# A two-layer decoder trunk on one core: the shared key's product before the first pooled-input tile, copies of the output stage ahead of weight splits, and three output tiles by ScalarE and an accumulating DMA

## The chip, the cores and the metric

One Trainium2 chip; the program runs on one of its NeuronCores. The time is that of one execution on the device, in microseconds (us). Before the change three timed runs took 782.8, 783.03 and 785.17 us, median 783.03. A further execution, the one that was profiled, took 781.9 us. About 0.3% (2.3 us) is what a measurement of this kernel can tell from no change.

Engine names: PE is TensorE's matmul stream, PEld its weight loads, ACT is ScalarE, DVE is VectorE, POOL is GpSimd, SP is SyncE, which here only issues DMAs.

## The reference

Two layers (DEPTH = 2), 512 tokens and 16 meta tokens ahead of them (T = 528), model width 1024, in float32. Per layer:

```
h = rmsnorm(x)
u_pool, z_pool, c_q, c_kv, k_rope, z_mla, g_pool, g_mla = split(h @ W_in)
y_pool = (PoolMix(u_pool) * silu(z_pool)) @ W_pool_up
y_mla  = (MLA(c_q, c_kv, k_rope) * silu(z_mla)) @ W_mla_up
x = x + (sigmoid(g_pool) * y_pool + sigmoid(g_mla) * y_mla) @ W_out
```

PoolMix subtracts u from causal running means over 2, 4, 8 and 16 tokens (four groups of 128 channels) and multiplies each group by a 128x128 matrix (`pool_w_group`, here `wgr`). MLA is causal attention of 8 heads; its rotary key k_rope (32 channels, here `kr`, weights `wkr`) is shared by all heads. Queries and keys are normalised per head.

## The kernel before, in words

**Layout.** Channels lie on the 128 partitions, tokens along the free dimension. The residual stream is `xb`, 8 tiles of 128x528. A product of full float32 accuracy is made by three fast passes: weight and activation are each split into a rounded high part and the rest, and `mm3` issues high*high, high*low, low*high (lines 192, 195, 196).

**The weight stream.** `stream()` runs through one long list, `plan`, of products of both layers, and cuts each weight into chunks of 512 columns. A chunk is loaded by SP into a tile `raw` (three buffers), ACT copies it, rounded, to `whi` (line 187), and DVE makes `wlo` = raw - whi (line 188). The load, the copy and the difference of a chunk are issued when PE's program has come to three chunks ahead. So the order of `plan` sets three things at once: PE's order, the order of SP's loads, and where the `whi` copies stand among the other work of ACT. Every engine works through its own list in order: an ACT instruction that waits holds up all that stand behind it on ACT.

**The products around the change.** Per layer the plan has cq0 to cq4 (query latents), then u0, k0, u1, kr, k1, u2, k2, u3, k3 (u: pooled input, k: keys of a pair of heads), then v, `yw` (the load and split of `wgr`, no product of its own; `hold` keeps the tiles), the zp and y tiles, cq5, and so on. Each cq and u tile has two weight chunks (c0, c1). The result of a cq tile is taken out of PSUM by ACT (line 714), by DVE (line 715) and by ACT again (a square into `tmp`, line 724), that of u by DVE times the norm `rinv` (line 550), that of k by DVE times `q` (line 749). PSUM banks of the tag `mm` go round four buffers, so a product's first matmul waits until the tile four earlier has been taken out. kr (lines 461 to 490) uses the raw weights with the gain multiplied in by POOL, 32 PE instructions of 32 rows, in two halves of the tokens; after its evacuation its later steps (`rest`) wait LAG of planned time.

**The norm.** `norm_sums` (from line 399) gets the norms of the layer's input as one column, and SP writes them to DRAM in four DMAs (`ndr<-ny`, lines 438 and 439, with one element per run), then reads them back spread over all partitions (`rinv<-ndr`, `q<-ndr`, line 444). These DMAs stand in SP's list between the weight loads.

**The output stage.** For each layer the tiles o0 to o3 are plain products of 8 chunks of K. After each half of the tokens `ev_o` (line 1092) adds 0.5 times the PSUM to `xb` on DVE, and `out` sends it on (in the last layer by a DMA to the output yT on POOL's queue). The other four tiles are made in two pairs (u = 0, 1) by seven half-size products instead of eight, in the order 1, 2, 7, 6, 5 ("oa"), o3, then 4, 3 ("ob"). Products 1, 6, 5 and 3 of a pair add up in one PSUM bank `S` and are read out between: after p = 1, 6 and 5 `carry` (line 1161) copies the bank to a tile `sv` by ACT (line 1163) and adds that to `xb` by an accumulating DMA that POOL issues (line 1164); the next product into the bank waits for that copy.

## Time and profile before

| what | us |
|---|---|
| timed runs, median of three | 783.03 (782.8 to 785.17) |
| the profiled execution | 781.9 |
| its span, first to last instruction | 780.1 |
| PE busy in the span | 773.2 |
| DVE, ACT, POOL busy | 569.7, 444.7, 232.7 |

The granted TensorE clock is 1.00 throughout. A row of a timeline gives start, duration, engine, line, operation, output <- inputs, shape, and in square brackets the idle time of that engine just before it and what ended it. The duration of a matmul row (0.28) is longer than the distance to the next row (0.12): matmuls are pipelined, so the distance counts. SPq and POOLq rows are the issues of DMAs, not their transfers; the DMA views give the time from issue to landing. Tiles are named without their numbers there: `raw`, `whi`, `mm` and so on.

### The profile page before, as it was taken

The numbers are of one execution on the slowest core, as the hardware profiler recorded it, in microseconds if no ns is written. First come the engines' busy times: TensorE is split into PE (matmuls) and PEld (weight loads), VectorE is DVE, ScalarE is ACT, GpSimd is POOL, SyncE is SP. The second block draws the span as 40 slices with busy tenths as digits, with TensorE's granted clock in tenths as the row PEclk, the third lists the DMA queues.
The fourth block names the chain that finished last, engine by engine and source line by source line (L and its number), as shares of the span: only waits on it lengthen the run. The fifth ranks groups of instructions, "written<-read, shape, count | busy, mean of one in ns | idle before, by whom it ended". The sixth has DMA issues, their size and how long they took to land.

```text
span 780.1 us, 15325 instructions
## 1 busy us (share of the span) xinstructions
PE 773.2 (99%) x5469; PEld 710.9 (91%) x5469; DVE 569.7 (73%) x1326; ACT 444.7 (57%) x1016; POOL 232.7 (30%) x303
## 2 busy tenths in 40 slices
PE   9999999999999999999999999999999999999998
PEld 8999899999999999999997898887788999988887
DVE  5848787446778876589764577866897888864994
ACT  7645555645566665645564446546657766664552
POOL 1024525103335333211330136221006625340213
PEclk9999999999999999999999999999999999999999
DMA  6232457765646465565662424425557666662645
GB/s 245 82 96 89 125 171 151 177 168 144 156 110 164 116 141 120 156 156 184 169 171 82 109 75 122 133 62 178 146 132 167 173 187 158 175 226 72 210 137 154
DMA packets 65325, 112.92 MB, mean 145 GB/s; under 512 B 10704, under 2 KB 15696, under 8 KB 65248
## 3 DMA queue, kind: packets, MB, share of 16 engines
q1 hardware_dynamic: 55344, 92.18, 39.1%
q0 software_dynamic: 8896, 17.92, 12.9%
q10 hardware_dynamic: 1008, 1.84, 0.7%
q8 instruction: 43, 0.70, 0.4%
q14 instruction: 34, 0.28, 0.1%
HBM read 100.18 MB, written 22.62 MB: 157 GB/s over the span
## 4 chain that ended last, share of the span: by engine, by line
PE 91%; DVE 4%; DMA 2%; ACT 1%; issue 1%; POOL 0%; DVEq 0%; ACTq 0%; POOLq 0%
PE mm L192 26%; PE mm L196 26%; PE mm L195 25%; PE S L195 3%; PE S L196 3%; PE S L192 3%; PE mm L979 2%; DVE wlo L188 1%; PE o L985 1%; PE o L984 1%; PE S L506 1%; DMA raw<-wgr 1%; DMA xb<-xT 1%; PE mm L408 1%; ACT whi L187 0%
## 5 line engine op out<-in xcount | busy, mean ns | idle before, releaser
L192 PE MATMUL mm<-hh,whi 128*128 128x264 f32 (+2 forms) x992 | 306.2, 311 | 0.5 <-DVE u L550 0.4
L196 PE MATMUL mm<-hh,wlo 128*128 128x264 f32 (+2 forms) x992 | 304.4, 309 | 0.1
L195 PE MATMUL mm<-hl,whi 128*128 128x264 f32 (+2 forms) x992 | 304.1, 308 | 0.0
L188 DVE TENSOR_TENSOR wlo<-raw,whi 128x512 fp32r<-128x512 f32 (+1 forms) x253 | 180.0, 714 | 100.3 <-ACT whi L187 98.0
L187 ACT ACTIVATE whi<-raw 128x512 fp32r<-128x512 f32 (+1 forms) x253 | 154.2, 613 | 168.7 <-PE mm L195 110.2
L192 PEld LDWEIGHTS mm<-hh,whi 128*128 128x128 f32 x992 | 186.2, 188 | 11.3 <-issue 1.0
L195 PEld LDWEIGHTS mm<-hl,whi 128*128 128x128 f32 x992 | 186.8, 188 | 8.7
L196 PEld LDWEIGHTS mm<-hh,wlo 128*128 128x128 f32 x992 | 185.9, 188 | 9.0 <-DVE wlo L188 0.6
L922 POOL TENSOR_SCALAR pa<-pa,rs 128x272 f32<-128x272 f32 (+1 forms) x32 | 33.2, 1038 | 103.3 <-DVE rs L941 64.5
L922 POOL TENSOR_SCALAR cq<-cq,rs 128x400 f32<-128x400 f32 (+1 forms) x32 | 51.2, 1600 | 0.0
L192 PE MATMUL mm<-cq,whi 128*128 128x264 f32 (+2 forms) x140 | 43.8, 313 | 0.0
L195 PE MATMUL mm<-cq,whi 128*128 128x264 f32 (+2 forms) x140 | 43.7, 312 | 0.0
L196 PE MATMUL mm<-cq,wlo 128*128 128x264 f32 (+2 forms) x140 | 43.3, 312 | 0.1
L908 DVE CUSTOM_DVE_ANT_0 S<-S,maskw,nqs 128x272 f32<-128x272 f32 (+4 forms) x80 | 38.6, 498 | 5.3 <-PE S L196 5.0
L725 POOL TENSOR_TENSOR racc<-racc,tmp 128x264 f32<-128x264 f32 (+1 forms) x15 | 14.0, 936 | 85.5 <-ACT tmp L724 85.5
L304 DVE TENSOR_TENSOR tl<-mm,th 128x512 fp32r<-128x512 f32 (+1 forms) x64 | 30.0, 483 | 8.0 <-ACT th L303 6.3
L359 POOL DMA_DIRECT2D wsum<-wout x8 | 7.0, 875 | 91.6 <-PE mm L196 86.9
L303 ACT ACTIVATE th<-mm 128x512 fp32r<-128x512 f32 (+1 forms) x64 | 26.3, 433 | 10.2 <-PE mm L979 9.6
L915 ACT ACTIVATE cq<-S,bia 128x400 f32<-128x400 f32 (+2 forms) x48 | 24.5, 514 | 13.2 <-DVE bia L953 8.5
L192 PE MATMUL mm<-u,whi 128*128 128x264 f32 (+1 forms) x96 | 31.3, 326 | 0.0
L196 PE MATMUL mm<-u,wlo 128*128 128x264 f32 (+1 forms) x96 | 30.9, 322 | 0.0
L195 PE MATMUL mm<-kn,whi 128*128 128x264 f32 (+1 forms) x96 | 30.6, 320 | 0.0
(344 smaller groups left out, 1684.7 us busy)
## 6 DMA issues: line engine op xcount, KB each, us to landing
raw<-win SPq DMA_DIRECT2D x139, 256.0 KB, 2.8
raw<-wout SPq DMA_DIRECT2D x22, 256.0 KB, 3.6
bc<-kdr SPq DMA_DIRECT2D x16, 264.0 KB, 4.5
wsum<-wout SPq DMA_DIRECT2D x16, 256.0 KB, 3.5
raw<-wpu SPq DMA_DIRECT2D x16, 256.0 KB, 2.7
wsumgp<-win SPq DMA_DIRECT2D x16, 256.0 KB, 3.4
raw<-wmu SPq DMA_DIRECT2D x16, 256.0 KB, 2.8
raw<-wsumgp SPq DMA_DIRECT2D x16, 256.0 KB, 4.3
```

The lines of the kernel that those rows point to most:

```text
L187: act.activation(hi[:, :n], raw[:, :n], AF.Copy)
L188: dve.tensor_sub(lo[:, :n], raw[:, :n], hi[:, :n].bitcast(F32))
L192: first = pe.matmul(out, wh, xh, start=start, stop=False, skip_group_check=more)
L195: pe.matmul(out, wh, xl, start=False, stop=False, skip_group_check=more)
L196: newest[0] = pe.matmul(out, wl, xh, start=False, stop=stop, skip_group_check=more)
L303: act.activation(hi[:, a:b], src, AF.Copy)
L304: dve.tensor_sub(lo[:, a:b], src, hi[:, a:b].bitcast(F32))
L725: self.acc_last = gp.tensor_add(self.acc[:, a:b], self.acc[:, a:b], t[:, :b - a])
L908: dve.tensor_tensor_reduce(out=sv, in0=sv, in1=mask, scale=nqs[:, i, h:h + 1], scalar=3e38, op0=ALU.add, op1=ALU.min, accum_out=bia[:, c:c ...
L915: act.activation(pv, sv, AF.Exp, scale=-1.0, bias=bia[:, i:i + 1], accum_out=rs[:, c:c + 1])
L922: gp.tensor_scalar(pt[i], pt[i], rs[:, i:i + 1], None, op0=ALU.mult)
L979: pe.transpose(tr[:, P * (i - j):P * (i - j + 1)], pt[i][:, NM + P * j:NM + P * (j + 1)], ident)
```

## The change

Four edits:

1. **kr** goes from behind u1 to ahead of u0 in the plan of both layers, and its later steps wait KR_LAG = 10500 instead of LAG = 2000 of planned time.
2. **yw** goes from behind v to behind u2; `wgr` is loaded into a buffer of the tag `bc` instead of the next `raw`, and its load waits for the newest matmul.
3. **The copies of p = 1** (`kept`, both layers): the second and third `whi` copies recorded after such a copy are made to stand behind it (`urgent`, `behind`). Its accumulating DMA (`join`) is now issued after the addition of p = 2 to the same tile.
4. **o0, o1, o2 of the last layer**: ACT copies 0.5 times the PSUM to a `tmp` tile, and POOL issues an accumulating DMA of it to `xb`, in place of DVE's addition.

```diff
@@ -53,6 +53,7 @@
 FILL = (2950.0, 2700.0)
 RESERVE = ("gm5", "gm5")
 LAG = 2000.0
+KR_LAG = 10500.0
 SPL = 240
 RET = 12500.0
 WARM = 8
@@ -169,8 +170,15 @@
             return self.src[c // 512] if isinstance(self.src, list) else self.src[:, c:c + n]
 
     loads = [0]
+    urgent = []
 
     def wload(src, n, gain, spare, buf=None, held=False):
+        if held:
+            hi, lo = slot("sv", F32R, bufs=2), slot("sv", F32R, bufs=2)
+            raw = slot("bc", bufs=3)
+            behind(sp.dma_start(raw[:, :n], src), newest[0])
+            split(hi, lo, raw[:, :n], 0, n)
+            return hi, lo
         raw = early.pop(0) if early else fetch(src, n, buf or rawt(), sp)
         loads[0] += 1
         pool, th, tl, nb = (tp, "th", "tl", 2) if loads[0] <= 2 or spare else (wp, "whi", "wlo", 3)
@@ -178,13 +186,13 @@
             v = raw[:, :n].rearrange("p (k m) -> p k m", k=8)
             gp.tensor_mul(v, v, gain.unsqueeze(2).to_broadcast([P, 8, n // 8]))
             return raw, None
-        if held:
-            hi, lo = slot("sv", F32R, bufs=2), slot("sv", F32R, bufs=2)
-            split(hi, lo, raw[:, :n], 0, n)
-            return hi, lo
         hi = pool.tile([P, W if pool is tp else 512], F32R, tag=th, name=nm("whi"), bufs=nb)
         lo = pool.tile([P, W if pool is tp else 512], F32R, tag=tl, name=nm("wlo"), bufs=nb)
-        act.activation(hi[:, :n], raw[:, :n], AF.Copy)
+        made = act.activation(hi[:, :n], raw[:, :n], AF.Copy)
+        for e in urgent:
+            e[1] += 1
+            if 1 < e[1] < 4:
+                behind(made, e[0])
         dve.tensor_sub(lo[:, :n], raw[:, :n], hi[:, :n].bitcast(F32))
         return hi, lo
 
@@ -487,7 +495,7 @@
                 act.activation(kr, t[:, :n], AF.Copy, scale=self.g(G_KR))
                 self.rope(self.kp[:, a:b], kr, a, b)
 
-            after(LAG, rest)
+            after(KR_LAG, rest)
 
         def stat(self, q, a, b, c, made):
             for s, (fa, fb) in enumerate(FULL):
@@ -1089,7 +1097,12 @@
         def ev_o(self, m, nxt):
             def ev(ps, a, b):
                 x = xb[:, m, a:b]
-                dve.scalar_tensor_tensor(out=x, in0=ps, scalar=0.5, in1=x, op0=ALU.mult, op1=ALU.add)
+                if self.last and m < 3:
+                    t = tmp()[:, a:b]
+                    act.activation(t, ps, AF.Copy, scale=0.5)
+                    gp.dma_start(x, t, accum_op=ALU.add)
+                else:
+                    dve.scalar_tensor_tensor(out=x, in0=ps, scalar=0.5, in1=x, op0=ALU.mult, op1=ALU.add)
                 self.out(m, (a, b), nxt, gp)
                 if not self.last and m == 3 and b == T:
                     nxt.square_x(m)
@@ -1158,10 +1171,15 @@
                 x = xb[:, m, s[0]:s[1]]
                 dve.scalar_tensor_tensor(out=x, in0=v, scalar=0.5, in1=x, op0=ALU.mult, op1=ALU.add)
 
+            def kept(v, u, scale, o):
+                urgent.append([act.activation(self.carried[u][:, o:o + n], v, AF.Copy, scale=scale), 0])
+
+            def join(m, s, u, o):
+                gp.dma_start(xb[:, m, s[0]:s[1]], self.carried[u][:, o:o + n], accum_op=ALU.add)
+
             def carry(m, s, v, u, scale, o):
-                t = self.carried[u][:, o:o + n]
-                act.activation(t, v, AF.Copy, scale=scale)
-                gp.dma_start(xb[:, m, s[0]:s[1]], t, accum_op=ALU.add)
+                kept(v, u, scale, o)
+                join(m, s, u, o)
 
             def body(i, w):
                 p, u = order[i]
@@ -1180,9 +1198,10 @@
                 q = sp if name == "ob" else gp
                 if p == 1:
                     self.carried[u] = slot("sv", bufs=2)
-                    carry(m0, A, ps, u, 0.5, 0)
+                    kept(ps, u, 0.5, 0)
                 elif p == 2:
                     grow(m0, A, ps)
+                    join(m0, A, u, 0)
                     self.out(m0, A, nxt, q)
                 elif p == 7:
                     grow(m1, B, ps)
@@ -1232,8 +1251,11 @@
                 cq(m)
             for m in range(4):
                 add(f"u{m}", wi(MT_U + m), D, evac=self.ev_u(m), xs=hs, segs=FULL)
-                if m == 1:
-                    add("kr", wkr[l], 256, body=self.kr_body, gain=gn[:, l * N_GAIN + G_H:l * N_GAIN + G_H + 8])
+                if m == 2:
+                    add("yw", wgr[l], 512, body=self.hold)
+                    plan[-1].held = True
+                if m == 0:
+                    plan.insert(-1, Gemm((l, "kr"), wkr[l], 256, body=self.kr_body, gain=gn[:, l * N_GAIN + G_H:l * N_GAIN + G_H + 8]))
                 kk(m)
             def zp(m):
                 add(f"zp{m}", wi(MT_ZP + m), D, evac=self.ev_silu(self.zps, "xa", m), xs=hs, segs=XS)
@@ -1242,8 +1264,6 @@
                 add(f"y{m}", None, P, body=self.y_body(m))
 
             add("v", wvb[l], 1024, body=self.v_body)
-            add("yw", wgr[l], 512, body=self.hold)
-            plan[-1].held = True
             zp(0)
             zp(1)
             y(0)
```

Lines of the changed file lie further down by 1 to 22 (whi copies 191, wlo 196, the cq evacuation 722, 723 and 732, kr 473, `rest` 492 on, the p = 1 copies 1175, o copies 1102).

What this makes of the order is shown at three places. In the names the first number counts the tiles of the program and the second the order of creation. The first place is SP's list in layer 0, around the norm's writes. Here raw_115 is chunk c1 of cq4. Before, raw_120 and raw_127 are u0's chunks c0 and c1:

```order
L115 DMA raw_115_706<-win 128x512
L115 DMA raw_120_738<-win 128x512
L438 DMA ndr00_115<-ny2_76_461 128x4x1
L439 DMA ndr00_115<-ny2_76_461 16x1
L438 DMA ndr01_116<-ny2_76_461 128x4x1
L439 DMA ndr01_116<-ny2_76_461 16x1
L115 DMA raw_127_780<-win 128x512
L444 DMA rinv_78_480<-ndr00_115 128x528
L444 DMA q1_79_481<-ndr01_116 128x528
L115 DMA raw_132_812<-wkb 128x256
```

Now, with u0's chunks as raw_125 and raw_134, and k0's as raw_139:

```order
L116 DMA raw_115_706<-win 128x512
L116 DMA raw_120_738<-wkr 128x256
L446 DMA ndr00_115<-ny2_76_461 128x4x1
L447 DMA ndr00_115<-ny2_76_461 16x1
L446 DMA ndr01_116<-ny2_76_461 128x4x1
L447 DMA ndr01_116<-ny2_76_461 16x1
L116 DMA raw_125_777<-win 128x512
L452 DMA rinv_78_480<-ndr00_115 128x528
L452 DMA q1_79_481<-ndr01_116 128x528
L116 DMA raw_134_813<-win 128x512
L116 DMA raw_139_845<-wkb 128x256
```

The load of kr's weights has taken the place ahead of the norm's writes; u0's two chunks have each moved one load back, u0's first chunk to behind the writes, and u0's second to behind the norm's reading back.

The second place is ACT's list at the same point of the program. mm_104 and mm_105 are the two halves of cq3, mm_118 and mm_119 those of cq4. Before:

```order
L724 ACTIVATE tmp_113_686<-mm_104_634 128x264
L187 ACTIVATE whi_121_740<-raw_120_738 128x512
L714 ACTIVATE cq6_111_682<-mm_105_635,gn_76 128x264
L724 ACTIVATE tmp_114_703<-mm_105_635 128x264
L187 ACTIVATE whi_128_782<-raw_127_780 128x512
L714 ACTIVATE cq8_123_756<-mm_118_712,gn_76 128x264
L724 ACTIVATE tmp_125_760<-mm_118_712 128x264
L187 ACTIVATE whi_133_814<-raw_132_812 128x256
L714 ACTIVATE cq8_123_756<-mm_119_713,gn_76 128x264
L724 ACTIVATE tmp_126_777<-mm_119_713 128x264
```

Now:

```order
L732 ACTIVATE tmp_113_686<-mm_104_634 128x264
L191 ACTIVATE whi_126_779<-raw_125_777 128x512
L722 ACTIVATE cq6_111_682<-mm_105_635,gn_76 128x264
L732 ACTIVATE tmp_114_703<-mm_105_635 128x264
L191 ACTIVATE whi_135_815<-raw_134_813 128x512
L722 ACTIVATE cq8_121_753<-mm_118_712,gn_76 128x264
L732 ACTIVATE tmp_123_757<-mm_118_712 128x264
L191 ACTIVATE whi_140_847<-raw_139_845 128x256
L722 ACTIVATE cq8_121_753<-mm_119_713,gn_76 128x264
L732 ACTIVATE tmp_124_774<-mm_119_713 128x264
L484 ACTIVATE tmp_131_794<-mm_128_783 128x264
L484 ACTIVATE tmp_133_808<-mm_132_799 128x264
```

The evacuations of cq3's second half and of cq4 keep their places; the `whi` copies ahead of each of them are now of a load that stands one further back in SP's list, and kr's own evacuation (L484) follows behind them all. On PE the halves of kr (mm_128, mm_132) and of u0 (mm_137, mm_138) take the PSUM banks of mm_104, mm_105, mm_118 and mm_119 in this order, so they wait for tmp_113, tmp_114, tmp_123 and tmp_124.

The third place is ACT's list in the last layer's output stage, around the copies of p = 1 (S_1959 and S_1964 before, S_1962 and S_1967 now). Before:

```order
L187 ACTIVATE whi_1971_10084<-raw_1970_10082 128x512
L303 ACTIVATE sq_1914_9831<-cq4_1871_9599 128x256
L187 ACTIVATE whi_1975_10105<-kh_1974_10103 128x512
L187 ACTIVATE whi_1983_10145<-kl_1982_10143 128x512
L303 ACTIVATE sq_1918_9835<-cq5_1872_9601 128x256
L303 ACTIVATE sq_1922_9839<-cq6_1856_9557 128x256
L187 ACTIVATE whi_1979_10125<-raw_1978_10123 128x512
L1163 ACTIVATE sv_1960_10036<-S_1959_10023 128x256
L1163 ACTIVATE sv_1965_10058<-S_1964_10045 128x256
L303 ACTIVATE rinv_1926_9843<-cq7_1876_9627 128x256
L187 ACTIVATE whi_1986_10165<-raw_1985_10163 128x512
```

Now, where kl_1969 holds the weights of p = 2 for u = 1, raw_1973 and kh_1977 those of p = 7, and mm_1954 is o2:

```order
L1102 ACTIVATE tmp_1958_10019<-mm_1954_9976 128x512
L311 ACTIVATE rinv_1926_9843<-cq7_1876_9627 128x256
L1175 ACTIVATE sv_1963_10042<-S_1962_10029 128x256
L1175 ACTIVATE sv_1968_10063<-S_1967_10050 128x256
L191 ACTIVATE whi_1970_10067<-kl_1969_10065 128x512
L191 ACTIVATE whi_1974_10089<-raw_1973_10087 128x512
L191 ACTIVATE whi_1978_10111<-kh_1977_10109 128x512
L191 ACTIVATE whi_1982_10131<-raw_1981_10129 128x512
```

Before, the two copies stood behind the weights of p = 7 (whi_1971, whi_1975) and of p = 6 (whi_1983, whi_1979); now they stand ahead of those (whi_1974, whi_1978, whi_1982) and of p = 2 for u = 1 (whi_1970), and behind the copy of o2.

## Prediction on record

> **What bounds the kernel now.** The page's busy times first, then the waits of PE:
>
> ```profile
> PE 773.2 (99%) x5469; PEld 710.9 (91%) x5469; DVE 569.7 (73%) x1326; ACT 444.7 (57%) x1016; POOL 232.7 (30%) x303
> ```
> ```profile
> PE S L192 <- ACT sv L1163: 1.1, 1, 1.1
> PE mm L192 <- DVE u L550: 0.8, 2, 0.4
> ```
>
> PE works in 773.2 of 780.1 us and waits in very few places. So an edit can win only what PE waits for there, and can lose whatever new wait it puts into a stream that has hardly any. Where PE waits, by its timeline:
>
> ```profile
> 58.09 0.28 PE L196 MATMUL mm<-kh,wlo 128*128 128x264 f32 x1
> 58.80 0.36 PE L192 MATMUL mm<-hh,whi 128*128 128x264 f32 x1 [0.42 <-DVE u L550]
> ...
> 83.58 0.40 PE L196 MATMUL mm<-whi,kl 128*128 128x512 f32 x1
> 84.38 0.50 PE L192 MATMUL mm<-whi,kh 128*128 128x512 f32 x1 [0.41 <-DVE u L550]
> ...
> 476.03 0.40 PE L196 MATMUL mm<-whi,kl 128*128 128x512 f32 x1
> 476.48 0.50 PE L192 MATMUL mm<-whi,kh 128*128 128x512 f32 x1
> ...
> 755.73 0.28 PE L196 MATMUL mm<-hh,wlo 128*128 128x256 f32 x1
> 757.08 0.39 PE L192 MATMUL S<-cq,whi 128*128 128x256 f32 x1 [1.07 <-ACT sv L1163]
> ```
>
> Distances count, less the usual one (0.12 us for 264 or 256 columns, 0.23 for 512): u1 loses 0.59 us, v 0.57 in layer 0 and 0.21 in layer 1, p = 6 of the last output stage 1.23. **Together 2.6 us: that is all the change can win, 0.33%.** The stall at 84.38 hangs on the load of wgr, as the chain of waits shows:
>
> ```profile
> 79.42 2.87 DMA raw<-wgr
> ```
>
> **Edit 1, kr ahead of u0, layer 0.** PE's work itself stays: kr takes 2.0 us wherever it stands.
>
> ```profile
> 64.86 1.99 PE L465 MATMUL mm<-xb,raw 128*32 128x264 f32 x32
> ```
>
> But every weight load from u0 on moves one place back in SP's list, and this is past the norm's writes. SP and ACT there:
>
> ```profile
> 38.93 0.33 SPq L115 DMA_DIRECT2D raw<-win  x1
> 40.10 0.39 SPq L438 DMA_DIRECT2D ndr<-ny  x1
> ...
> 42.15 0.37 SPq L115 DMA_DIRECT2D raw<-win  x1
> ...
> 49.88 0.32 SPq L444 DMA_DIRECT2D q<-ndr  x1
> 50.29 0.38 SPq L115 DMA_DIRECT2D raw<-wkb  x1
> ```
> ```profile
> 47.05 0.39 ACT L724 ACTIVATE tmp<-mm 128x264 f32<-128x264 f32 x1 [1.02 <-DVE cq L715]
> 52.54 0.63 ACT L187 ACTIVATE whi<-raw 128x512 fp32r<-128x512 f32 x1 [5.10 <-DMA raw<-win]
> 53.08 0.47 ACT L714 ACTIVATE cq<-mm,gn 128x264 fp32r<-128x264 f32 x1
> 54.40 0.39 ACT L724 ACTIVATE tmp<-mm 128x264 f32<-128x264 f32 x1 [0.85 <-DVE cq L715]
> 54.69 0.41 ACT L187 ACTIVATE whi<-raw 128x256 fp32r<-128x256 f32 x1
> ```
>
> The load issued at 42.15, right behind the writes, is not there before 52.5, 10.4 us later, and ACT stands still for 5.1 us. The writes, of single elements, need 8.6 us from issue to landing themselves:
>
> ```profile
> ndr<-ny SPq DMA_DIRECT2D x2, 2.0 KB, 8.6
> ```
>
> Today this costs PE nothing: the late load is u0's second chunk, and cq3 has left its PSUM bank by 47.44, ahead of the hold. After the change the late load is u0's **first** chunk, its copy stands on ACT ahead of the second evacuation of cq3, and kr's second half needs that bank. With the row distances above moved to the new order:
> - PE ends cq4 at 50.79, where u0 starts today:
>
> ```profile
> 50.79 0.28 PE L192 MATMUL mm<-hh,whi 128*128 128x264 f32 x1
> ```
>
> - kr's first half runs 50.9 to 51.85 (its bank was free long ago). The copy of u0's first chunk starts at 52.54, the evacuation of cq3 behind it ends at 54.79 (54.40 + 0.39). kr's second half starts at 54.9: **3.0 us of PE idle**.
> - u0's second chunk is issued at 50.29 and lands at 54.3, as the load issued at 50.29 does today:
>
> ```profile
> DMA to landing us min/median/max: 4.0/4.0/4.0
> ```
>
>   Its copy goes 54.9 to 55.5, then cq4's first half is taken out: today's stretch from the start of a whi copy to the end of the tmp behind it is 52.54 to 54.79, 2.25 us, so 57.1. kr ended at 55.85: **1.3 us idle** before u0.
> - k0's load waits for the raw buffer of u0's first chunk (DVE's difference ends near 53.9), lands near 57; copy and evacuation of cq4's second half (2.25 us again, less 0.2 since the copy is 256 wide, 0.41 against 0.63) end near 59.1. u0's first twelve matmuls, 0.12 apart, end at 58.6: **0.5 us**.
>
> Together 4.8 us; the 0.59 us of u1 goes (ACT has caught up, some 3 us, when u1 starts): **+4.2 us**. Bounds: -0.59, if the load lands by 49.6 (51.85 less 2.25), and +6, if it lands 1.8 us later still.
>
> **Edit 1, layer 1.** The same list, with all of the evacuation in one piece of 512:
>
> ```profile
> 435.34 0.37 SPq L115 DMA_DIRECT2D raw<-win  x1
> ```
> ```profile
> 444.45 0.94 ACT L187 ACTIVATE whi<-raw 128x512 fp32r<-128x512 f32 x2 [3.35 <-DMA raw<-win]
> 445.30 0.67 ACT L714 ACTIVATE cq<-mm,gn 128x512 fp32r<-128x512 f32 x1
> 446.90 0.60 ACT L724 ACTIVATE tmp<-mm 128x512 f32<-128x512 f32 x1 [0.93 <-DVE cq L715]
> ```
>
> Here cq4 ends at 443.98 and kr finds free banks: 444.0 to 446.0. u0's first half waits for cq3's evacuation, now behind the copy at 444.45: about 2.7 us on (its copy 0.54, then 445.30 to 447.50 as shown, less the second copy), 447.15: 1.15 us idle. Its second half waits for cq4's, behind the copy of k0's weights, whose load can be issued only when DVE has used the late chunk, near 445.85. The view of the loads issued from 445.8 to 446.7 has one of this size whose landing it shows, that of wkr:
>
> ```profile
> DMA to landing us min/median/max: 3.1/3.1/3.1
> ```
>
> So 448.9, and 2.5 us from the k0 copy (near 445.0 today) to 447.50, gives 451.4 at most; with a landing after 2.0 us 450.4. u0's first twelve end at 448.6: 1.8 to 2.8 us idle, taken as 2.15. **+3.3 us**, bounds 0 and +4.2.
>
> **Edit 2, yw.** wgr takes 2.87 us to land (the chain's row above) and is now asked for after u2's first chunk. Its split stands on ACT ahead of u3's second chunk, which PE needs 60 matmuls later (24 of u2, 12 of k2, 24 of u3), 7.2 us. Both stalls at v go: **-0.78 us**; at worst as much comes back (0).
>
> **Edits 3 and 4, last output stage.** ACT's copies of p = 1 come late because they stand behind a whi copy that waits; PE's last matmul of the banks, then ACT:
>
> ```profile
> 754.52 0.28 PE L196 MATMUL S<-hh,wlo 128*128 128x256 f32 x1
> ```
> ```profile
> 756.12 0.63 ACT L187 ACTIVATE whi<-raw 128x512 fp32r<-128x512 f32 x1 [1.57 <-PE mm L196]
> 756.66 0.64 ACT L1163 ACTIVATE sv<-S 128x256 f32<-128x256 f32 x2
> ```
>
> With the banks complete near 754.7, the copies put in front end at 755.4, and the 1.23 us go; but now the weights of p = 2 (u = 1) are copied behind them, 755.4 to 756.05, and are wanted at 755.85, their differences 0.65 later, and those of p = 7 follow as closely: 0.7 us come back. On PE -0.5. Then POOL: three accumulating DMAs of 0.88 us issue more, and each output DMA behind waits for their landing (median 3.5 us at half the size):
>
> ```profile
> xb<-sv POOLq DMA_DIRECT2D x6, 128.0 KB, 3.5
> ```
> ```profile
> 764.97 0.88 POOL L1164 DMA_DIRECT2D xb<-sv  x1
> ...
> 774.27 0.56 POOL L1101 DMA_DIRECT2D yT<-xb  x1 [1.04 <-DMA xb<-sv]
> ```
> ```profile
> 773.41 4.32 SPq L1101 DMA_DIRECT2D yT<-xb  x4
> ```
>
> One after the other (o1 asked for near 751.3, three such rounds of 4 to 6 us, then p = 5's two, o3's output last) they bring POOL's last output issue from 774.3 to about 777.4, just where SP's last issue is today (773.41 plus 4.32 us for four). So POOL takes the 0.5 us back: **0**, bounds -1.2 and +2.5. DVE's three additions of 0.68 us that go stood beside other work. In layer 0's output stage, where PE has no wait now, the new order is taken at **+0.3** (0 to +1).
>
> **Sum.** 4.2 + 3.3 - 0.8 + 0 + 0.3 = +7.0 us. The profiled execution (span 780.1, 781.9 in all, the rest as before) becomes 788.9. It was 1.1 us below the median of the timed runs, 783.03, from which it would be 790.0. I say **789.0**, nearer to the first, whose rows made the sum.
>
> **The rivals.**
> - *The load isn't held, faster.* If u0's first chunk lands like others (the page's median for raw<-win is 2.8 us) before 49.6 in layer 0 and 443.3 in layer 1, ACT is in time everywhere, all four stalls go and 781.9 - 2.6 = **779.3**. Against: two loads in exactly this place took 10.4 and 9.1 us. For: other orders of the same bytes haven't been seen. 12%.
> - *Only one layer pays.* Layer 1's kr finds its banks free, so it has 2 us more than layer 0; if the loads there land 3 us sooner, its 3.3 go and **785.6** remains; half of both holds gives 781.9 + 7.5/2 - 0.5 = 785.2, a third 783.9. Together, with the case that little moves (781 to 783: the new waits in the output stages eat what yw gives), 18%.
> - *PE slows after the idle.* At the start of the span PE's matmuls of 264 columns are still 0.22 us apart, instead of 0.12:
>
> ```profile
> 5.71 0.42 PE L195 MATMUL S<-hl,whi 128*128 128x264 f32 x1
> 5.93 0.34 PE L196 MATMUL S<-hh,wlo 128*128 128x264 f32 x1
> ```
>
>   If an idle of 3.0 us brings that back for as long as at the start (1.0 to 5.9), 4.9 x (1 - 0.12/0.22) = 2.2 us more: **791.2**, from an idle that long on. The longest idle in mid-run today, 1.07 us at 757.08, has no such aftermath. 12%. The Trainium skill, "TensorE: Matmul & The Clock Gate", section "HAM oscillation — how this bites in real kernels", warns of idle gaps over about 3.4 us, after which the clock is halved; by it a gap of 3.0 us, followed after 1 us of narrow matmuls by one of 1.3, lies at the edge. The page's granted clock of 1.00 even at the start doesn't show it; the distances do.
>
> **How the numbers follow.** The forecast with its own range 785.5 to 791 has 58%; the slow PE 12%; little or half the loss 18%; the free load 12%. Faster by over 0.3% (under 780.7): 0.12. Within 0.3%, about what a measurement can tell from no change: 0.18. Slower (over 785.4): 0.70. The range leaves out the free load and the ends of the others: 782.0 to 792.5.
>
> **What would show it.** Right: ACT idle some 5 us to a DMA raw<-win near 52.5, with the cq evacuation behind it; PE idle near 3 us in the middle of kr, near 55, and again before u0, both ended by ACT's tmp; in layer 1 two waits within u0, at 447 and 451; no wait at v; p = 6 without its 1.1 us, and POOL's issues ending near SP's. Wrong: u0's first load landing before 50, or PE's idle put down to POOL or to kr's own weights.

## The result, and the profile after

The changed kernel took **791.69 us** (median of six runs, 790.14 to 794.54), beside 782.91 us (six runs, 781.74 to 785.17) for the kernel before. The ratio is **1.0113 [1.0091, 1.0135]**: 8.8 us slower, 7.1 to 10.6 by the interval. The forecast of 789.0 had the sign, 7.0 of the 8.8 us, and the place. The profiled execution of after is the slowest of its six, 794.54 us with a span of 792.5; some of what follows in its trace is therefore its own, and is named as such.

The page's busy times of after. PE does the same 5469 instructions, and its share falls from 99% to 98%; ACT has three copies more and DVE three additions less.

```profile
PE 778.2 (98%) x5469; PEld 714.0 (90%) x5469; DVE 565.9 (71%) x1323; ACT 447.4 (56%) x1019; POOL 233.8 (30%) x306
```

PE's waits in after (total, times, longest). What stood here before, the waits for `sv` and for `u`, is gone or small; in their place PE waits for ACT's `tmp`, the evacuation of cq:

```profile
PE mm L200 <- ACT tmp L732: 4.6, 3, 2.3
PE mm L473 <- ACT tmp L732: 2.0, 1, 2.0
PE mm L987 <- POOL pa L930: 1.2, 1, 1.2
...
PE mm L200 <- DVE u L558: 0.3, 1, 0.3
```

SP's list in layer 0 of after. The load at 43.33 is u0's first chunk, directly behind the four writes of the norm; `q` is read back only at 51.53, and u0's second chunk is asked for behind it, at 51.95.

```profile
40.12 0.33 SPq L116 DMA_DIRECT2D raw<-wkr  x1
41.28 0.38 SPq L446 DMA_DIRECT2D ndr<-ny  x1
...
42.73 0.50 SPq L447 DMA_DIRECT2D ndr<-ny  x1
43.33 0.37 SPq L116 DMA_DIRECT2D raw<-win  x1
49.10 0.33 SPq L452 DMA_DIRECT2D rinv<-ndr  x1
51.53 0.32 SPq L452 DMA_DIRECT2D q<-ndr  x1
51.95 0.38 SPq L116 DMA_DIRECT2D raw<-win  x1
54.24 0.33 SPq L116 DMA_DIRECT2D raw<-wkb  x1
```

ACT at the same place: 6.58 us idle until that load is there, and then each evacuation of cq (L732) one behind a weight copy (L191) that came late.

```profile
45.89 0.39 ACT L732 ACTIVATE tmp<-mm 128x264 f32<-128x264 f32 x1 [0.62 <-DVE cq L723]
52.86 0.63 ACT L191 ACTIVATE whi<-raw 128x512 fp32r<-128x512 f32 x1 [6.58 <-DMA raw<-win]
53.39 0.46 ACT L722 ACTIVATE cq<-mm,gn 128x264 fp32r<-128x264 f32 x1
54.71 0.39 ACT L732 ACTIVATE tmp<-mm 128x264 f32<-128x264 f32 x1 [0.85 <-DVE cq L723]
56.24 0.63 ACT L191 ACTIVATE whi<-raw 128x512 fp32r<-128x512 f32 x1 [1.14 <-DMA raw<-win]
...
58.09 0.39 ACT L732 ACTIVATE tmp<-mm 128x264 f32<-128x264 f32 x1 [0.85 <-DVE cq L723]
```

PE: kr is cut into two halves, with 2.00 us idle between them and 2.28 us behind them. Then the first matmuls of u0 follow each other after 0.39 and 0.22 us, not after 0.12.

```profile
52.06 1.10 PE L473 MATMUL mm<-xb,raw 128*32 128x264 f32 x16
55.15 1.10 PE L473 MATMUL mm<-xb,raw 128*32 128x264 f32 x16 [2.00 <-ACT tmp L732]
58.53 0.59 PE L200 MATMUL mm<-hh,whi 128*128 128x264 f32 x1 [2.28 <-ACT tmp L732]
58.92 0.42 PE L203 MATMUL mm<-hl,whi 128*128 128x264 f32 x1
59.14 0.42 PE L204 MATMUL mm<-hh,wlo 128*128 128x264 f32 x1
```

The windows of the same stretch (busy time and count of PE, PEld, DVE, ACT and POOL, then the granted clock, the DMA share and GB/s). The clock is 0.50 for the 3 us after the second idle, and back at 1.00 from 62 on:

```profile
55.10:58.50 3.40, 1.10 (x16) 0.42 (x16) 1.09 (x2) 1.41 (x5) 0.75 (x1) 0.98 0.15 51
58.50:60.00 1.50, 1.47 (x6) 1.47 (x7) 1.18 (x2) 0.66 (x2) 0.75 (x1) 0.50 0.50 175
60.00:61.00 1.00, 1.00 (x7) 1.00 (x6) 0.20 (x2) 0.85 (x3) 0.32 (x1) 0.50 0.11 43
61.00:62.00 1.00, 1.00 (x7) 1.00 (x7) 0.97 (x3) 0.11 (x1) 0.43 (x1) 0.60 0.86 305
62.00:63.00 1.00, 1.00 (x10) 1.00 (x9) 0.97 (x4) 0.00 (x0) 0.00 (x0) 1.00 0.13 45
```

Layer 1: kr runs in one piece, and u0 waits twice, ahead of its first half and ahead of its second. The clock stays at 1.00 here.

```profile
450.87 1.99 PE L473 MATMUL mm<-xb,raw 128*32 128x264 f32 x32
454.65 0.39 PE L200 MATMUL mm<-hh,whi 128*128 128x264 f32 x1 [1.79 <-ACT tmp L732]
...
458.32 0.39 PE L200 MATMUL mm<-hh,whi 128*128 128x264 f32 x1 [0.56 <-ACT tmp L732]
```

How much each place costs is read by pairing each PE instruction of after with the same one of before and taking the difference of their starts, in the two profiled executions. It grows by 1.3 us in the first 10 us of the span (PE's matmuls stay 0.22 us apart to 10.5 us instead of 6); by 5.0 at kr and u0 of layer 0, the 0.59 us that u1 no longer waits included; it falls by 0.6 at v; grows by 0.2 up to the attention, by 0.9 in layer 0's output stage, by 3.3 at kr and u0 of layer 1; falls by 0.2 at v; grows by 1.2 at one attention step that waited for POOL (line 987 above), by 0.6 up to 662, and by 0.2 in the last output stage. Together 12.0; the span grew by 12.4. Without the start and the attention's wait, 9.5 remain, near the 8.8 of the medians; both are taken for chance. The profile of the kernel with u0's weights ahead (below) has the same attention wait at no loss, and a kernel with all four edits and constant products (below) has 0.2 us there; the profile of the kernel with edits 1 and 2 and u0's weights ahead has the same slow start, also at no loss.

### The profile page after: what moved, and what is told of

Same layout as the page of the kernel before. It is cut to its first block, busy times and chain, and to the rows that moved or that the text cites. A ratio compares the mean times of both kernels' runs of the same rounds, so it can differ in the third digit from the quotient of the medians.

```text
span 792.5 us, 15331 instructions
## 1 busy us (share of the span) xinstructions
PE 778.2 (98%) x5469; PEld 714.0 (90%) x5469; DVE 565.9 (71%) x1323; ACT 447.4 (56%) x1019; POOL 233.8 (30%) x306
## 4 chain that ended last, share of the span: by engine, by line
PE 86%; DVE 5%; DMA 4%; ACT 2%; issue 2%; POOL 1%; SPq 0%; DVEq 0%; ACTq 0%
PE mm L200 24%; PE mm L204 24%; PE mm L203 24%; PE S L203 2%; PE S L204 2%; PE S L200 2%; PE mm L987 2%; DVE wlo L196 2%; PE o L993 1%; DMA ndr<-ny 1%; PE o L992 1%; DMA raw<-win 1%; ACT whi L191 1%; PE S L514 1%; DMA raw<-wsum 1%
## 5 line engine op out<-in xcount | busy, mean ns | idle before, releaser
L200 PE MATMUL mm<-hh,whi 128*128 128x264 f32 (+2 forms) x992 | 307.6, 313 | 5.5 <-ACT tmp L732 4.6
L196 DVE TENSOR_TENSOR wlo<-raw,whi 128x512 fp32r<-128x512 f32 (+1 forms) x253 | 178.2, 708 | 115.8 <-ACT whi L191 113.7
L191 ACT ACTIVATE whi<-raw 128x512 fp32r<-128x512 f32 (+1 forms) x253 | 154.1, 613 | 164.8 <-PE mm L203 106.6
L200 PEld LDWEIGHTS mm<-hh,whi 128*128 128x128 f32 x992 | 187.2, 190 | 18.2 <-ACT tmp L732 5.8
L930 POOL TENSOR_SCALAR cq<-cq,rs 128x400 f32<-128x400 f32 (+1 forms) x32 | 54.7, 1728 | 0.0
L200 PE MATMUL mm<-cq,whi 128*128 128x264 f32 (+2 forms) x140 | 43.8, 313 | 0.0
L200 PE MATMUL mm<-u,whi 128*128 128x264 f32 (+1 forms) x96 | 31.3, 327 | 0.0
```

The source lines that it names most:

```text
L191: made = act.activation(hi[:, :n], raw[:, :n], AF.Copy)
L196: dve.tensor_sub(lo[:, :n], raw[:, :n], hi[:, :n].bitcast(F32))
L200: first = pe.matmul(out, wh, xh, start=start, stop=False, skip_group_check=more)
L930: gp.tensor_scalar(pt[i], pt[i], rs[:, i:i + 1], None, op0=ALU.mult)
```

## The experiments

Every time is a median beside runs of the kernel before on the same chip (781.47 to 781.74 there). The ratio goes by the means of the runs, so it can differ a little from that of the medians; differences in us are worked out from the ratio. In brackets is its interval.

**Which edit.** First each side of the cut: edit 1 alone, and all but edit 1.

*Edit 1 alone*, on the kernel before:

```diff
-            after(LAG, rest)
+            after(10500.0, rest)
...
-                if m == 1:
-                    add("kr", wkr[l], 256, body=self.kr_body, gain=...)
+                if m == 0:
+                    plan.insert(-1, Gemm((l, "kr"), wkr[l], 256, body=self.kr_body, gain=...))
```

> The kernel before with edit 1 alone. Theory H: 791 to 793, all of the loss plus the 0.8 us that edit 2 would win. Theory O: 786 to 789. In the trace under H: PE idle 2.0 to 3.0 us in the middle of kr and over 2 us ahead of u0 in layer 0, 1.8 and 0.6 us within layer 1's u0, and a granted clock of 0.5 for some 3 us behind the second idle.

Measured 789.86 us, ratio 1.0108 [1.0091, 1.0125], +8.4 us: between the ranges of the two theories, nearer to H. The profile is of the fastest of its four executions, 787.22 us. In it PE waits for the same two things, at the same places (1.42 us in the middle of kr, 2.32 ahead of u0 in layer 0), and the granted clock falls to 0.50 behind them:

```profile
PE mm L192 <- ACT tmp L724: 3.6, 3, 2.3
PE mm L465 <- ACT tmp L724: 1.4, 1, 1.4
```

Edit 1 by itself makes a loss as large as the whole change makes.

*Edit 1 undone*, on the changed kernel (kr behind u1 and LAG again, edits 2 to 4 kept):

```diff
-            after(KR_LAG, rest)
+            after(LAG, rest)
...
-                if m == 0:
-                    plan.insert(-1, Gemm((l, "kr"), wkr[l], 256, body=self.kr_body, gain=...))
+                if m == 1:
+                    add("kr", wkr[l], 256, body=self.kr_body, gain=...)
```

> The change with edit 1 undone: kr behind u1 and its late steps after LAG, as before; edits 2 to 4 stay. Theory H (the loss is edit 1's alone: the held load of u0's first chunk on ACT, then PE): the time falls to 781.5 to 783, since the 0.78 us at v are won and the output stages come out even; no PE wait between 51 and 60 us, ACT's idle of 5 us stays ahead of u0's second chunk. Theory O (part of the loss sits in the output stages or in POOL's accumulating DMAs): 784 to 787. Theory A (the lost time after layer 0's kr is mostly chance of the profiled execution): also near 782.

Measured 783.53 us, ratio 1.0024 [1.0015, 1.0033], +1.9 us. No wait for `tmp` is left. But the other edits were to give 0.5 us, and they lose 1.9; the time lies above the range of theory H. The trace says where: PE's last matmul starts at 777.5 (before: 776.6), and the span goes on to 782.1 (before: 780.1). So 0.9 us are PE's, and 1.1 are the tail behind it: the chain that ends last now runs through POOL, which asks for its last output DMAs only from 776.88 on (before: 774.27), behind the accumulating ones.

```profile
771.67 2.67 POOL L1178 DMA_DIRECT2D xb<-sv  x3
776.88 1.77 POOL L1114 DMA_DIRECT2D yT<-xb  x3 [2.54 <-DMA xb<-sv]
```

**Why edit 1 costs.** The forecast's reason was the load held up behind the norm's writes. Three kernels vary that hold.

*The norm's writes issued by POOL*, so that SP's queue holds only the loads:

```diff
-                sp.dma_start(row[0, NM:T].rearrange("(j p) -> p j", p=P), ny[:, i, 0:4])
-                sp.dma_start(row[0, 0:NM].rearrange("(p j) -> p j", j=1), ny[0:NM, i, 4:5])
+                gp.dma_start(row[0, NM:T].rearrange("(j p) -> p j", p=P), ny[:, i, 0:4])
+                gp.dma_start(row[0, 0:NM].rearrange("(p j) -> p j", j=1), ny[0:NM, i, 4:5])
```

> The change with the four norm writes of each layer issued from POOL instead of SP, so that they stand in another DMA queue than the weight loads; nothing else. Theory Hq (u0's first load is late because it stands behind the small writes in the same queue): it lands within 3 to 5 us of its issue near 41, ACT takes cq3 out before 48, no idle in layer 0's kr, and in layer 1 none ahead of u0: 782 to 785. Theory He (the small writes hold the DMA engines themselves, whichever queue they are in): the load lands near 52 again, and the time stays at 790 to 793.

Measured 806.99 us, ratio 1.0326 [1.0311, 1.0342], +25.5 us, which no theory had. SP, POOL and ACT in layer 0:

```profile
41.15 0.33 SPq L116 DMA_DIRECT2D raw<-win  x1
...
58.20 0.33 SPq L452 DMA_DIRECT2D q<-ndr  x1
58.62 0.38 SPq L116 DMA_DIRECT2D raw<-wkb  x1
```
```profile
40.00 0.91 POOL L446 DMA_DIRECT2D ndr<-ny  x1 [2.36 <-DVE ny L325]
40.90 0.54 POOL L447 DMA_DIRECT2D ndr<-ny  x1
48.11 0.81 POOL L446 DMA_DIRECT2D ndr<-ny  x1 [6.67 <-issue]
```
```profile
50.17 0.63 ACT L191 ACTIVATE whi<-raw 128x512 fp32r<-128x512 f32 x1 [5.47 <-DMA raw<-win]
...
63.54 0.42 ACT L191 ACTIVATE whi<-raw 128x256 fp32r<-128x256 f32 x1 [8.12 <-DMA raw<-wkb]
```

Two things are seen. u0's first chunk, asked for at 41.15, is used only at 50.17, 9.0 us on, though the writes now stand in another queue: so it isn't SP's order that holds the load, but something that the queues share. The bytes themselves are late, not only the sign that they are there. The windows (columns as above) show a load of the same size ahead of the writes, in before (issued at 38.93), then u0's first chunk behind them in after, up to where the next read begins, and the same chunk here:

```profile
39.90:41.20 1.30, 1.30 (x12) 1.30 (x12) 0.54 (x2) 1.27 (x3) 0.76 (x1) 1.00 0.68 202
44.30:51.00 6.70, 6.70 (x57) 6.70 (x56) 1.36 (x2) 0.87 (x2) 1.07 (x2) 1.00 0.31 36
42.10:49.80 7.70, 7.70 (x65) 7.70 (x65) 1.18 (x2) 1.25 (x3) 1.67 (x3) 1.00 0.32 34
```

Ahead of the writes the 256 KB go through in 1.3 us, at 202 GB/s; behind them they trickle in at 36 and 34 GB/s, whichever queue the writes are in.

And a new loss: POOL could not issue the second pair of writes until 48.11, 6.67 us later, in which it waited for nothing that the profile shows; so `q` was read at 58.20 and the weights of k0 behind it came at 63.5. The Trainium skill, "DMA: Bandwidth & Descriptors", section "Queues, rings and completion order", says that the semaphore of a DMA is raised by a write that lands only after every earlier write of the same DMA engine, across its queues. The order of landings here is in keeping with it: the first pair of writes landed 7.8 and 7.1 us after 40.00 and 40.90, ahead of the load. But it is not what the load waited for in the end, since its bytes were still moving until 49.8.

*kr one place later*, between u0 and k0, on the changed kernel:

```diff
-                    plan.insert(-1, Gemm((l, "kr"), wkr[l], 256, body=self.kr_body, gain=...))
+                    add("kr", wkr[l], 256, body=self.kr_body, gain=...)
```

> The change with kr one product later, between u0 and k0, still with KR_LAG; edits 2 to 4 stay. SP's list up to u0's second chunk is then that of the kernel before, and the late load is again the second chunk of u0. Theory H: PE has no idle ahead of u0 and 782 to 784.5 come out. If the loss came from kr standing early as such (its two tmp tiles held for KR_LAG, or DVE's work for it behind u0), it would stay above 787.

Measured 784.66 us, ratio 1.0039 [1.0024, 1.0054], +3.1 us, just above the range of theory H. u0's first chunk is again ahead of the writes; PE's waits for `tmp` of cq are gone, its clock is 1.00, and two small waits stand there instead:

```profile
PE mm L200 <- DVE tmp L486: 1.0, 1, 1.0
PE mm L200 <- ACT whi L191: 0.5, 1, 0.5
```

Moving kr ahead of k0 and u1 costs about 1.2 us beside the same kernel with kr at its old place (ratio 1.0024); moving it ahead of u0 as well costs some 7. The step comes where u0's first chunk goes behind the norm's writes.

*u0's weights ahead of the writes*, with kr where the change puts it. The order of SP's list is what the theory blames, so this takes away the hold of u0's chunks and leaves PE's order: they are loaded ahead of the writes into two tiles that are free then (`u2`, `kn2`), which also spares two of the `raw` buffers.

```diff
+            if g_.name[1] == "u0":
+                early.append(layers[g_.name[0]].pre.pop(0))
...
+            for c, t in ((0, slot("u2", w=WU)), (512, slot("kn2"))):
+                behind(sp.dma_start(t[:, 0:512], win[self.l, MT_U][:, c:c + 512]), mm)
+                self.pre.append(t)
             for i, d in enumerate((self.inv, self.cinv)):
```

> The change with u0's two weight chunks of each layer loaded into two free tiles, with their issue ahead of the norm writes in SP's list; kr stays ahead of u0, all else as in the change. Theory H: the load right behind the writes is now that of k0's weights, ACT takes cq3 and the first half of cq4 out without a hold, PE has no idle in the middle of kr and none ahead of u0, at most 1 us within u0 (the second half of cq4 stands behind k0's copy): 783 to 785.5, close to the change with kr put back (783.5 beside 781.5 of before). If kr ahead of u0 costs by itself (its tmp tiles, DVE's and POOL's work), it stays above 787.

Measured 781.86 us beside 781.66, ratio 1.0005 [0.9996, 1.0014]: the whole loss is gone, and more than theory H expected. PE and ACT in layer 0; the copies of u0's chunks (from `u` and `kn` now) come at 45.35 and 48.30, and kr runs unbroken into u0:

```profile
51.21 1.99 PE L478 MATMUL mm<-xb,raw 128*32 128x264 f32 x32
53.12 0.39 PE L200 MATMUL mm<-hh,whi 128*128 128x264 f32 x1
```
```profile
45.35 0.63 ACT L191 ACTIVATE whi<-u 128x512 fp32r<-128x512 f32 x1
...
48.30 0.63 ACT L191 ACTIVATE whi<-kn 128x512 fp32r<-128x512 f32 x1 [0.54 <-PE mm L203]
```

With this the cause of the loss is shown, not only argued: the same PE order costs nothing that can be measured once the late load is no longer u0's. (It is now k0's, asked for at 42.47 and copied at 51.24, and PE does not wait for it.) By like instructions PE gains 0.8 us at kr, u0 and u1 in this trace and 0.9 at v, and gives back 0.85 in layer 0's output stage, 1.2 at the attention step and 0.5 in the last stage.

**The half clock.** After the two idles of layer 0 the granted clock fell. Two kernels keep PE busy there, with products of a constant that no one reads.

*Six 128x128 products behind each half of kr*, on the changed kernel:

```diff
+                idle = pp.tile([P, 512], F32, tag="o", name=nm("wps"), bufs=1)
+                for _ in range(6):
+                    pre[0] = pe.matmul(idle[:, 0:P], ones, ones, start=True, stop=True)
+                    behind(pre[0], last)
```

> The change with six 128x128 products of constants, whose result nobody reads, behind each half of kr in both layers, placed where PE would be idle. The waits for ACT stay. Theory C (the granted clock of 0.5 behind the idle costs time of its own, 1.5 to 3 us an execution): the granted clock stays at 1.000 and the time falls 1 to 3 us below the change, 787 to 789.5 beside 781.5 of before. Without theory C, the same time as the change, 790 or more.

Measured 793.22 us, ratio 1.0149 [1.0135, 1.0163], slower than the change itself. The clock did stay at 1.00 from 52 to 64. But the work that was added moved the order on ACT: u1's first weight copy came to stand behind the last copies of kr, and PE got a new wait, `PE mm L200 <- DVE u L567`, of 3.1 us together in two places. So this run says nothing about the clock's price; the next one mends it.

*The same, with kr's last copies held behind u1's first weight copy*:

```diff
-                act.activation(kr, t[:, :n], AF.Copy, scale=self.g(G_KR))
+                if a == 0:
+                    self.kw = whis[-2]
+                behind(act.activation(kr, t[:, :n], AF.Copy, scale=self.g(G_KR)), self.kw)
```

> The change with constant products behind the halves of kr once more, and kr's last copy on ACT held behind u1's first weight copy, so that ACT's list is nearly that of the change (with the busy products before, the weight copy had moved behind kr's copies and u1 waited 1.6 us for DVE). Theory C: granted clock 1.000 and 1 to 2.5 us less than the change, 788 to 789.5 beside 781.5 of before. If u1 then waits for the evacuations anyway, no less than the change, 790.5 or more: the half clock is then hidden behind ACT and DVE.

Measured 789.95 us, ratio 1.0105 [1.0092, 1.0119], between the ranges of the two cases. The clock is 1.00 and the new wait is gone. A window of layer 0 (columns as above), and the first matmul of u0's second half:

```profile
58.00:61.00 3.00, 2.65 (x22) 2.44 (x21) 2.07 (x6) 1.43 (x4) 0.75 (x1) 1.00 0.43 137
```
```profile
58.88 0.39 PE L201 MATMUL mm<-hh,whi 128*128 128x264 f32 x1 [0.34 <-ACT tmp L744]
```

By like instructions, kr and u0 of layer 0 cost 3.7 us here and 5.0 in the profile of after: the half clock is worth about 1 us in these two traces. The trace of edit 1 alone is a closer neighbour: there u0 begins at 56.80, as here, and u1 at 65.61 against 64.84, 0.8 us later. By the medians the ratio overlaps that of the change, so its price isn't resolved. The rest of the loss stays, as it must if the late load makes it.

**Where edits 2 to 4 lose.** Each by itself or with one other, on the kernel before.

*Edit 2 alone* (yw behind u2, in its own buffer; its lines as in the change).

```diff
+                if m == 2:
+                    add("yw", wgr[l], 512, body=self.hold)
+                    plan[-1].held = True
...
-            add("yw", wgr[l], 512, body=self.hold)
-            plan[-1].held = True
```

> Edit 2 alone on the kernel before. It should win the two stalls at v, 0.8 us: 780.4 to 781.2 beside 781.5, a ratio of 0.9985 to 0.9997. If the earlier load and split of wgr disturb u3 or k3 as much, 781.5 or more.

Measured 781.34 us beside 781.66, ratio 0.9998 [0.9989, 1.0007]: no gain that can be measured. In its trace PE gains 0.57 us at v in layer 0 and 0.21 in layer 1, as forecast; 0.8 us is hardly more than the interval's 0.7 us either way.

*Edits 2 and 3*:

```diff
+            def kept(v, u, scale, o):
+                urgent.append([act.activation(self.carried[u][:, o:o + n], v, AF.Copy, scale=scale), 0])
...
-                    carry(m0, A, ps, u, 0.5, 0)
+                    kept(ps, u, 0.5, 0)
...
+                    join(m0, A, u, 0)
```

> Edits 2 and 3 alone: kr in its old place, o0 to o2 of the last layer by DVE again. Theory T (the 2 us that edits 2 to 4 lose come from the accumulating DMAs of o0 to o2, whose landings hold POOL, which then ends last): 780.5 to 782, 1.5 to 2.5 us below the change with kr put back, and POOL's last output issue near 775 in the trace. Rival (they come from the copies put ahead of the weight copies in both output stages): 783 or more.

Measured 782.78 us beside 781.66, ratio 1.0019 [1.0010, 1.0028], +1.5 us (the medians are 1.1 apart), between the ranges of theory T and its rival. With edit 2 alone at 0.9998, edit 3 costs rather than gains. Against the kernel before, its trace has 0.9 us of small delays in layer 0's output stage (from 379.4 on, 0.2 at a time), and four waits of 0.40, 0.26, 0.18 and 0.18 us in the last stage in place of the 1.23: the weight copies that now stand behind the copies of p = 1 come late for p = 2, 7 and 6.

*Edit 4 alone*:

```diff
-                dve.scalar_tensor_tensor(out=x, in0=ps, scalar=0.5, in1=x, op0=ALU.mult, op1=ALU.add)
+                if self.last and m < 3:
+                    t = tmp()[:, a:b]
+                    act.activation(t, ps, AF.Copy, scale=0.5)
+                    gp.dma_start(x, t, accum_op=ALU.add)
+                else:
+                    dve.scalar_tensor_tensor(out=x, in0=ps, scalar=0.5, in1=x, op0=ALU.mult, op1=ALU.add)
```

> Edit 4 alone on the kernel before: o0 to o2 of the last layer by ACT and accumulating DMAs. If POOL's later end makes the execution longer (its last output issue near 778 against SP's near 777.4): 782 to 783 beside 781.6. If PE's end decides: 781.4 to 781.8, the 1.2 us wait for the copies of p = 1 still there.

Measured 786.63 us beside 781.74, ratio 1.0065 [1.0052, 1.0078], +4.9 us: far more than expected. Its POOL and DVE, and the windows (columns as above):

```profile
758.93 0.55 POOL L1106 DMA_DIRECT2D yT<-xb  x1 [3.54 <-DMA xb<-tmp]
759.56 1.85 POOL L1169 DMA_DIRECT2D xb<-sv  x2
```
```profile
764.78 0.42 DVE L1164 SCALAR_TENSOR_TENSOR xb<-mm,xb 128x256 f32<-128x256 f32 x1 [4.19 <-DMA xb<-sv]
```
```profile
760.00:764.00 4.00, 1.52 (x13) 1.31 (x12) 0.59 (x2) 1.85 (x5) 1.41 (x2) 0.93 0.93 246
764.00:768.00 4.00, 2.74 (x7) 2.16 (x8) 2.56 (x5) 0.00 (x0) 2.43 (x4) 0.50 0.29 63
```

POOL waits 3.54 us for the last `tmp` to be added before it can send o2 on; only then, at 759.56, does it issue the accumulating DMAs of p = 1. DVE's addition of p = 2 to the same tile waits 4.19 us for them, PE waits 3.7 us for DVE, and the clock falls to 0.50 within this wait and stays there behind it. In the changed kernel this doesn't happen, since edit 3 issues these DMAs (`join`) behind the addition of p = 2. So edit 4 hangs on edit 3.

**What can be won.** If the late load is the only thing in kr's way, kr's new place with u0 ahead of the writes, and edit 2, should win some of what PE waits for.

*Edits 1 and 2 with u0's weights ahead* (the diffs above together, without edits 3 and 4):

> The kernel before with edits 1 and 2 and u0's chunks loaded ahead of the norm writes; without edits 3 and 4. From the runs so far: with all four edits and these loads 781.86 beside 781.66 of before, and edits 3 and 4 cost about 1.5 us more than they win: 779.5 to 780.8, a ratio of 0.997 to 0.999, faster than both kernels. If edits 3 and 4 cost nothing and the loss of edits 2 to 4 is of another kind, 781.5 to 782.5.

Measured 781.36 us beside 781.74, ratio 1.0000 [0.9991, 1.0009]: no gain that can be measured, and less than expected. In its trace PE gains the 0.8 us at v; the interval, 0.7 us either way, doesn't resolve so little.

*u0's weights ahead alone*, on the kernel before:

> The kernel before with u0's chunks loaded ahead of the norm writes and no edit of the change. If the gain of that (the 0.59 us that u1 waits behind the held copies) is independent of kr's place: 780.8 to 781.3 beside 781.6, and no wait of u1 at 58.8. If kr ahead of u0 has a gain of its own once its load isn't held, this is slower than the same loads with edits 1 and 2 by 1 us or more.

Measured 782.32 us beside 781.74, ratio 1.0007 [0.9998, 1.0016]. In its trace u1's wait is gone, as expected (its first matmul follows at 58.24, 0.12 us behind the one before), but the time is not below that of the kernel before, and lies above the 780.8 to 781.3 expected: 0.59 us is less than the interval's 0.7 either way. No kernel of this study beats the one before by more than its interval.

## Why the prediction was right, and where it was off

**The bound.** The change could win 2.6 us at most, since PE waits for little else. The stalls at v went, as forecast (0.57 and 0.21 us in the trace). No run came out faster than before, so none contradicts the bound and none comes near it: with the loss taken away (u0's weights ahead of the writes) the time is level with before, not the 779.3 of the rival in which the load isn't held, since in its trace what PE wins goes again in the output stages and at the attention step.

**Edit 1, layer 0: +4.2 forecast, +5.0 in the trace.** The mechanism is the one forecast, and is shown by three runs: edit 1 alone makes +8.4 us in both layers, u0's weights ahead of the writes takes it away, and without the move it doesn't arise. Its sizes were off in both directions:
- The idle in the middle of kr was put at 3.0 us and was 2.00. **The step that failed is the length of the late load, 10.4 us taken over from before.** Here it took 9.5 (issued 43.33, used 52.86), and in the trace of edit 1 alone 9.0 (42.13 to 51.09), with 1.42 us of idle. That PE was 1.3 us late from the start of the span (kr began at 52.06, where u0 began at 50.79 before) does not explain it: the load was asked for 1.2 us later too (43.33 against 42.15).
- The idle ahead of u0 was put at 1.3 and was 2.28. This is the other side of the same step: kr ended sooner than forecast, and u0 began where the forecast has it, at 57.1 and the late start of 1.3 us, 58.4, against 58.53. Together the two idles were put at 4.3 us and were 4.28. Within it, the forecast let u0's second chunk land before ACT was free; it was asked for at 51.95, behind the read of `q`, and ACT, free sooner for the same reason, waited 1.14 us for it.
- The 0.5 us within u0 did not show. Sixteen of its matmuls, not the "first twelve" of the forecast, stand ahead of its second half in the program's order, and PE had become slow: with the clock at 0.50 some fifteen stood 0.22 instead of 0.12 us apart, 15 x 0.10 = 1.5 us, for the 3 us from 58.5 on. This is the rival "PE slows after the idle". It came on top of the two idles and in place of the 0.5 us: where constant products kept the clock at 1.00, these show (58.88 there, 0.51 us more than the usual distance).

For that rival I had named the Trainium skill, "TensorE: Matmul & The Clock Gate", section "HAM oscillation — how this bites in real kernels", which warns of idle gaps over about 3.4 us. Here two gaps of 2.0 and 2.28 us, with 1.1 us of kr's narrow matmuls between, were followed by 0.50, and so were 1.42 and 2.32 us in the trace of edit 1 alone, while 1.79 us by itself in layer 1 was not, and neither were gaps near 1 us. Taken as one gap they would be over the figure; no run here tests gaps between 1.8 and 3.7 us that stand alone.

**Edit 1, layer 1: +3.3 forecast, +3.3 in the trace**, as 2.2 us ahead of u0's first half, 0.7 ahead of its second and 0.5 near 471, against 1.15 and 2.15 forecast. The sum was right by two errors that offset each other:
- The load came later against PE: issued at 442.14, it was used from 451.95, 0.9 us ahead of kr's end at 452.86; the forecast had 1.55 (444.45 and 446.0).
- **"u0's first twelve end at 448.6" was wrong**: 21 matmuls stand there, 9 x 0.12 = 1.1 us more, which hid as much of the second wait.

**Edit 2: -0.78 forecast, -0.78 in the trace.** Right.

**Edits 3 and 4: 0 and +0.3 forecast.** This is the term that was too small: +1.9 us by the kernel with edit 1 undone [1.2, 2.6], where edit 2 alone gives nothing measurable, and +1.5 of it are there with edits 2 and 3. In layer 0's output stage the new order of ACT cost 0.9, not 0.3. In the last stage the bound of +2.5 by POOL held. POOL's last three output issues began at 776.88 in the kernel with edit 1 undone, the last of them at 778.1, against the 777.4 forecast; that this ends the span behind PE, the forecast had priced at only the 0.5 us of PE's gain. In the profile of after the chain that ends last runs through PE and DVE as before, so there POOL's end is not what counts.

**The sum.** +7.0 against +8.8 [7.1, 10.6]. By the ratios edit 1 (+8.4) and the others (+1.9) give 10.3, more than both together; the intervals (8.4 by 1.3 either way, 1.9 by 0.7) leave it open whether they share something.

**What stays open.** Edits 3 and 4 cost about 1.9 us where kr is back, but with u0's weights ahead the kernel with all edits is only 0.05% above its neighbour, and that with edits 1 and 2 at 0.00%: 0.4 us. In the profiles of the kernel with edit 1 undone and of that with u0's weights ahead PE ends within 0.2 us of the same time, and the difference lies in the last 10 us, where POOL's order of accumulating DMAs and output DMAs hangs on landings of 2 to 7.6 us that differ between the traces; no run separates them. The exact price of the half clock is open as well, and so is why small writes slow down a load of another queue: the runs show that they do, and not by what. Writing the norm in fewer, longer runs, which would go at the root of the hold, was not tried.

## What to carry to other kernels

Where one order feeds several engines' queues, follow a moved step through each of them: kr cost PE nothing itself, but moved u0's weights behind four small DMAs that take about 8 us to land (7.3 to 9.0 in the trace), and their copy stood ahead of the evacuations that free the PSUM banks. The check on such a cause is to keep the new order and take away only the late transfer: here 1.0113 became 1.0005. And an edit that loses by itself (edit 3) can be what makes another bearable (edit 4, by the later `join`), so undo edits one at a time and in pairs before adding up their prices.

## What the runs showed of the hardware that was not expected

- Small writes hold up a load of another queue: with the norm's writes on POOL's queue the load of 256 KB on SP's still took 9.0 us (41.15 to 50.17), where the median of such loads is 2.8 us in before. Its bytes came at 34 GB/s, against 202 for a load ahead of the writes.
- POOL could not issue a second pair of these writes until 6.67 us after it had issued the first, without a wait that the profile shows.
- The granted clock fell to 0.50 with the second of two gaps of 2.0 and 2.28 us with 1.1 us of narrow matmuls between (for 3 us), with the second of 1.42 and 2.32 us (edit 1 alone), and within one of 3.7 us (edit 4 alone).
